# A third pair of k tiles by seven products in every second gate/up chunk, and the mixer's block transfers issued from SyncE

## The chip, the cores and the metric

The kernel runs on one core of a Trainium2 chip. The metric is device time in microseconds (us) of one execution. The core's engines are TensorE (PE in the profile; PEld its weight loads), VectorE (DVE), ScalarE (ACT), GpSimd (POOL) and SyncE (SP); each takes its instructions in the order in which the program lists them.

## The reference

One decoder layer on 256 positions of width 2048, all in float32:

```
x = x + 0.5 * swiglu(rms_norm(x, ffn1_norm), w_gate, w_up, w_down)      # 2048 -> 5632 -> 2048
h = rms_norm(x, mix_norm); proj = h @ w_in                               # 2048 -> 11776
dq, dk, dv, fq, fk, fv, g_dil, g_diff = split(proj)
o_dil  = mix of three dilated causal attention groups (4 heads each)
o_diff = causal differential attention (4 heads), normed
y = sigmoid(g_dil) * (o_dil @ W_A) + sigmoid(g_diff) * (o_diff @ W_B)
x = x + y @ w_out
x = x + 0.5 * swiglu(rms_norm(x, ffn2_norm), w_gate2, w_up2, w_down2)

def swiglu(h, w_gate, w_up, w_down):
    return (jax.nn.silu(h @ w_gate) * (h @ w_up)) @ w_down
```

## The kernel before

**Products in three parts.** TensorE multiplies in a rounded format. So each operand is split into a high part and a low part, and a product is three matmuls: high by high, high by low, low by high (`three`, L146 to L152). The activations `xh`, `xl` lie split in SBUF, 16 k tiles of 128. Weights come from memory in `raw` tiles of two k tiles by 512 columns (512 KB), loaded by SyncE; ScalarE writes the high part `w_hi` (L110, L125), VectorE subtracts it to get `w_lo` (L111, L126). There are five pairs of `w_hi` and `w_lo` buffers (`SPL_BUFS`), four `raw` buffers, and two more inside the feed-forward networks. A buffer is free when TensorE has done the matmuls that read it.

**Feed-forward.** Gate and up have 5632 columns: 11 chunks of 512, six in the first half and five in the second, each half followed by its share of the down product. Chunk 0 is done by `linear`, gate after up. Chunks 1 to 10 are done by `two_chunks` (L176): gate and up of a chunk together, over 8 pairs u of k tiles. A plain pair takes 8 products (2 k tiles, 2 blocks of 128 positions, 2 columns), from two split tiles of 1024 elements a partition. For the pairs in `sx` the 2 by 2 block product is done with seven products instead (a Winograd form of Strassen's scheme). They need sums of x, made once by `sums_of_x` (L154), and sums of weights, made at once on VectorE:

```
            b = parts(raw[0])
            three(p1, op(0, 0), part(b, 0), st, sp)
            three(c00, op(1, 0), part(b, 1), False, False)
            b = parts(raw[1][:, 1:], 1)
            three(c01, sm(3), part(b, 0), False, False)
            ... four subtractions on VectorE, in place in raw (L217 to L220)
            b = parts(raw[0])
            three(p5, sm(0), part(b, 0), st, sp)
            three(c10, op(1, 1), part(b, 1), False, False)
            b = parts(raw[1])
            three(p7, sm(2), part(b, 0), st, sp)
            three(p6, sm(1), part(b, 1), st, sp)
```

So such a pair has four split tiles: the first with 6 matmuls, the second (half a tile, 512 elements) with 3, the third and fourth, of the sums, with 6 each. `WINO = (3, 5)` names these pairs for gate and up, `WINO_DOWN = (3, 6)` those of the down product. After the last such pair four VectorE adds join the p sums (L231 to L234), after the chunk four more join the accumulators (L236); then come the gate products (L387) and two block transposes (L279). All eight PSUM banks are used, and chunks swap their roles.

**Transposing through memory.** The result of a chunk has to be turned so that its columns become k tiles. `turn_blocks` (L273) transposes 32 by 32 blocks on VectorE, writes them to memory (`blocks<-turned`, L281) and reads them back in another order (L284, into `moved`, or `q`, `fk`, `dk` in the mixer), both from GpSimd's queue. The read-back waits for the write to land. `split_blocks`, or `arrange` for the queries (L597), then takes it up some groups of weights later (`defer`).

**Mixer.** `qk_chunk` (L560) projects, norms and rotates queries and keys and turns them by `turn_blocks`; `turn_y` (L809) and `residual` (L408) do so for the mixer's output and for the new x. Their weights go through `linear`, and the norms need a power on GpSimd (L246).

**Order.** The program is written once through; a scheduler with a model of the engines' times then sets the order on each engine. So a change of the pairs also changes where VectorE's and ScalarE's other work stands.

Of the kernel before, what the change touches and what calls it, by code (L numbers as in the profile page):

```python
# [11 lines left out]
F32 = mybir.dt.float32  # L12
# [3 lines left out]
ALU = mybir.AluOpType  # L16
# [15 lines left out]
SPL_BUFS = 5  # L32
FFN_SPL = 0
FFN_RAW = 2
WINO = (3, 5)
WINO_DOWN = (3, 6)
HALVES = (6, 5)
DIL_G, DIL_H = 3, 4
# [17 lines left out]
def hybrid_layer_kernel(ctx: ExitStack, tc: tile.TileContext, a: dict, out: bass.AP):  # L56
# [94 lines left out]
        nc.tensor.matmul(ps, h, wl, start=False, stop=False)  # L151
        nc.tensor.matmul(ps, l, wh, start=False, stop=stop)  # L152

    def sums_of_x(pool, pairs, xh, xl, name):  # L154


        sx = {}
        for u in pairs:
            f = raw_tile()
            x, sm = f[:, 0].rearrange("p (k s) -> p k s", s=S), f[:, 1].rearrange("p (i m) -> p i m", m=P)  # L160
            nc.vector.tensor_tensor(x, xh[:, 2 * u:2 * u + 2].bitcast(F32), xl[:, 2 * u:2 * u + 2].bitcast(F32),
                                    op=ALU.add)
            a00, a01, a10, a11 = x[:, 0, :P], x[:, 1, :P], x[:, 0, P:], x[:, 1, P:]
            nc.vector.tensor_tensor(sm[:, 0], a10, a11, op=ALU.add)
            nc.vector.tensor_tensor(sm[:, 1], sm[:, 0], a00, op=ALU.subtract)
            nc.vector.tensor_tensor(sm[:, 2], a10, a00, op=ALU.subtract)
            nc.vector.tensor_tensor(sm[:, 3], a01, sm[:, 1], op=ALU.subtract)
            h, l = pool.tile([P, 4, P], F32R, name=f"{name}_h{u}"), pool.tile([P, 4, P], F32R, name=f"{name}_l{u}")
            nc.scalar.activation(h, sm, AF.Copy)
            nc.vector.tensor_tensor(l, sm, h.bitcast(F32), op=ALU.subtract)  # L170
            sx[u] = h, l
        return sx

    roles = itertools.count()
# [1 line left out]
    def two_chunks(cols, xh, xl, nk, sx, tmp):  # L176

        four = [ps_mm.tile([P, CH], F32, name="mm") for _ in range(4)]

        def other():
            tr = [ps_tr.tile([P, 2, S], F32, name="tr").rearrange("p a b -> p (a b)") for _ in range(2)]
            sc = ps_s.tile([P, 2, CH], F32, name="s")
            return [*tr, sc[:, 0], sc[:, 1]]

        (c00, c01, c10, c11), (p1, p5, p6, p7) = (four, other()) if next(roles) % 2 else (other(), four)
        c = ((c00, c01), (c10, c11))
        e, u2, x, y = (tmp.tile([P, CH], F32, name=n) for n in ("e", "u2", "x", "y"))  # L190
        nu, first_sum, last_sum = nk // 2, min(sx), max(sx)
        for u in range(nu):
            raw = []
            for w, n0 in cols:
                r = raw_tile()
                nc.sync.dma_start(r, w[2 * u * P:(2 * u + 2) * P, n0:n0 + CH].rearrange("(k p) n -> p k n", p=P))
                raw.append(r)
            op = lambda k, t: (xh[:, 2 * u + k, t * P:(t + 1) * P], xl[:, 2 * u + k, t * P:(t + 1) * P])
            if u not in sx:
                for i in range(2):  # L200
                    hi, lo = parts(raw[i])
                    for k in range(2):
                        for t in range(NT):
                            three(c[t][i], op(k, t), (hi[:, k], lo[:, k]), u == 0 and k == 0, u == nu - 1 and k == 1)
                    tick()
                continue
            st, sp = u == first_sum, u == last_sum
            sm = lambda i: (sx[u][0][:, i], sx[u][1][:, i])
            part = lambda hl, k: (hl[0][:, k], hl[1][:, k])

            (b00, b10), (b01, b11) = ([r[:, k] for k in range(2)] for r in raw)
# [5 lines that stand above are left out]
            nc.vector.tensor_tensor(b00, b01, b00, op=ALU.subtract)  # L217
            nc.vector.tensor_tensor(b01, b01, b11, op=ALU.subtract)
            nc.vector.tensor_tensor(b11, b11, b00, op=ALU.subtract)
            nc.vector.tensor_tensor(b10, b10, b11, op=ALU.subtract)  # L220
            tick()
# [6 lines that stand above are left out]
            tick()  # L228
            if sp:
                nc.scalar.activation(e, p1, AF.Copy)  # L230
                nc.vector.tensor_tensor(u2, p6, e, op=ALU.add)  # L231
                nc.vector.tensor_tensor(x, p5, u2, op=ALU.add)
                nc.vector.tensor_tensor(u2, p7, u2, op=ALU.add)
                nc.vector.tensor_tensor(y, p7, x, op=ALU.add)  # L234
        for acc, p in ((e, c00), (u2, c10), (x, c01), (y, c11)):
            nc.vector.tensor_tensor(acc, p, acc, op=ALU.add)  # L236
        return (e, x), (u2, y)
# [32 lines left out]
                for b in range(2):  # L270
                    split(xh[:, k + b], xl[:, k + b], tr[:, b], gains[:, k + b:k + b + 1])

    def turn_blocks(srcs, pool, x=None):  # L273

        r = pool.tile([P, 4, NT, 4, 32], F32, name="turned")
        for t in range(NT):
            nc.vector.transpose(r[:, :, t], srcs[t].rearrange("p (kt i q) -> p q kt i", i=32, q=4))  # L279
        d = dram.tile([4, P, NT * P], F32, name="blocks")  # L280
        nc.gpsimd.dma_start(d.rearrange("a (i q) x -> (a i) q x", q=4), r.rearrange("p q t kt j -> p q (t kt j)"))  # L281
        if x is None:
            x = pool.tile([P, 4, NT, 4, 32], F32, name="moved")
        nc.gpsimd.dma_start(x.rearrange("p a t kt j -> p a (t kt j)"), d.rearrange("a p x -> p a x"))  # L284
        return x

    def split_blocks(x, xh, xl, k0, gains=None):
# [73 lines left out]
    def ffn(wg, wu, wd, norm, done, ahead=None):  # L361
        with tc.tile_pool(name="act", bufs=1) as apool, tc.tile_pool(name="actw", bufs=1) as aw, \
                tc.tile_pool(name="actb", bufs=1) as bp, tc.tile_pool(name="acts", bufs=1) as sxp, \
                tc.tile_pool(name="actt", bufs=FFN_RAW) as wt, ExitStack() as spl:
            more_raw.append(wt)
            more_spl.append(spl)
            ah = apool.tile([P, 4 * HALVES[0], S], F32R, name="ah")
            al = apool.tile([P, 4 * HALVES[0], S], F32R, name="al")
            j = 0
            for half, count in enumerate(HALVES):  # L370
                down = wd[j * CH:(j + count) * CH]
                for i in range(count):
                    if j == 0:
                        ps = linear(wg, 0, xh, xl, KD, ahead)
                        rs = norm()
                        sg = [aw.tile([P, CH], F32, name=n) for n in ("e", "u2")]
                        for t in range(NT):
                            nc.scalar.activation(sg[t], ps[t], AF.Silu, scale=rs[t])
                        up = linear(wu, 0, xh, xl, KD)
                        sx = sums_of_x(sxp, WINO, xh, xl, "sx")  # L380
                    else:
                        out = two_chunks(((wg, j * CH), (wu, j * CH)), xh, xl, KD, sx, aw)
                        sg, up = [o[0] for o in out], [o[1] for o in out]
                        for t in range(NT):
                            nc.scalar.activation(sg[t], sg[t], AF.Silu, scale=rs[t])
                    for t in range(NT):
                        nc.vector.scalar_tensor_tensor(sg[t], up[t], rs[t], sg[t], op0=ALU.mult, op1=ALU.mult)  # L387
                    x = turn_blocks(sg, bp)
                    defer(BLOCK_WAIT, lambda x=x, i=i: split_blocks(x, ah, al, 4 * i))
                    j += 1  # L390
                sd = sums_of_x(sxp, WINO_DOWN, ah, al, "sd")
                for n in range(0, D // CH, 2):
                    if half and n == D // CH - 2:
                        break
                    y = two_chunks([(down, (n + c) * CH) for c in range(2)], ah, al, 4 * count, sd, aw)
                    for c in range(2):
                        (done if half else part)(n + c, [o[c] for o in y], bp)
                for n in range(D // CH - 2 if half else D // CH, D // CH):
                    done(n, linear(down, n * CH, ah, al, 4 * count), bp)
            more_spl.clear()  # L400
            more_raw.clear()
# [467 lines left out]
```

## Time and profile before

| | |
|---|---|
| runs (us) | 2123.31, 2119.55, 2126.64; median 2123.31 |
| profiled execution | 2119.51 us, span 2117.7 us |
| TensorE busy | 2102.6 us (99%), 9334 matmuls |
| VectorE busy | 1589.1 us (75%) |
| ScalarE busy | 1082.5 us (51%) |
| GpSimd busy | 100.2 us (5%) |
| weights and the rest from memory | 215 GB/s over the span |

TensorE is busy throughout; a kernel like this gets shorter by fewer matmuls or by fewer pauses of TensorE. A busy share of VectorE is a mean over stages: the feed-forward networks stand at about 50 to 720 and 1450 to 2118 us of the span, the mixer between them.

### The profile page before, as it was taken

The page shows a single profiled execution, that of the slowest core. Times are in us where ns is not written, and L with a number is a line of the kernel's source. Part 1 is how long each engine was busy: PE and PEld are TensorE (multiplying, and loading weights), DVE is VectorE, ACT ScalarE, POOL GpSimd, SP SyncE. Part 2 cuts the span into 40 slices and gives each one's busy share as a digit, 9 for nine tenths or more (in the row PEclk, how much of TensorE's full clock was granted, in tenths as well). Part 3 has the DMA queues.
Part 4 walks back from the last instruction along what each step waited for, and adds up shares of the span by engine and source line. Part 5 has one row for each costly group of instructions (what it writes and reads, how often), then busy time and mean ns, then how long its engine had stood idle before and what let it go on. Part 6 is the DMA issues. An engine that isn't in the chain of part 4 may idle for free.

```text
span 2117.7 us, 25700 instructions
## 1 busy us (share of the span) xinstructions
PE 2102.6 (99%) x9334; PEld 1736.9 (82%) x9334; DVE 1589.1 (75%) x2048; ACT 1082.5 (51%) x1335; POOL 100.2 (5%) x132
## 2 busy tenths in 40 slices
PE   9999999999999999999999999999999999999999
PEld 7888888888888888878888888888888888888887
DVE  6888987688898666677755556666898877888883
ACT  6555554455455545465555444554554544455542
POOL 1000000000000011011100000000000000000000
PEclk9999999999999999999999999999999999999999
DMA  8666665576668676766555667665676656567673
GB/s 282 218 216 210 224 236 188 186 242 227 215 209 275 224 232 196 237 190 216 192 188 159 207 223 250 228 224 179 227 241 214 210 207 218 196 218 233 207 251 125
DMA packets 224836, 456.29 MB, mean 215 GB/s; under 512 B 14098, under 2 KB 14660, under 8 KB 224452
## 3 DMA queue, kind: packets, MB, share of 16 engines
q1 hardware_dynamic: 212512, 411.09, 58.5%
q0 software_dynamic: 12096, 43.52, 6.4%
q8 instruction: 73, 1.20, 0.2%
q14 instruction: 55, 0.45, 0.1%
q10 hardware_dynamic: 100, 0.03, 0.0%
HBM read 428.89 MB, written 25.69 MB: 215 GB/s over the span
## 4 chain that ended last, share of the span: by engine, by line
PE 94%; DMA 2%; DVE 2%; ACT 1%; issue 1%; POOL 0%; ACTq 0%; POOLq 0%; DVEq 0%
PE mm L141 12%; PE mm L142 12%; PE mm L143 12%; PE mm L151 9%; PE mm L152 9%; PE mm L150 9%; PE tr L151 5%; PE tr L152 5%; PE tr L150 5%; PE s L150 5%; PE s L151 5%; PE s L152 5%; DMA q<-blocks 1%; DMA blocks<-turned 1%; DVE w_lo L126 1%
## 5 line engine op out<-in xcount | busy, mean ns | idle before, releaser
L110 ACT ACTIVATE w_hi<-raw 128x1024 fp32r<-128x1024 f32 (+1 forms) x560 | 553.0, 1016 | 540.8 <-DVE raw L220 183.7
L111 DVE TENSOR_TENSOR w_lo<-raw,w_hi 128x1024 fp32r<-128x1024 f32 (+1 forms) x560 | 639.4, 1170 | 163.1 <-ACT w_hi L110 161.0
L126 DVE TENSOR_TENSOR w_lo<-raw,w_hi 128x1024 fp32r<-128x1024 f32 (+1 forms) x313 | 378.9, 1218 | 259.5 <-ACT w_hi L125 256.6
L125 ACT ACTIVATE w_hi<-raw 128x1024 fp32r<-128x1024 f32 (+1 forms) x313 | 328.3, 1056 | 300.4 <-PE mm L143 250.0
L141 PE MATMUL mm<-w_hi,xh 128*128 128x512 f32 x864 | 339.2, 394 | 0.0
L142 PE MATMUL mm<-w_lo,xh 128*128 128x512 f32 x864 | 338.9, 393 | 0.0
L143 PE MATMUL mm<-w_hi,xl 128*128 128x512 f32 x864 | 336.7, 393 | 0.0
L151 PE MATMUL mm<-w_lo,xh 128*128 128x512 f32 x540 | 210.2, 389 | 0.0
L152 PE MATMUL mm<-w_hi,xl 128*128 128x512 f32 x540 | 210.1, 389 | 0.0
L150 PE MATMUL mm<-w_hi,xh 128*128 128x512 f32 x540 | 201.0, 389 | 0.0
L142 PEld LDWEIGHTS mm<-w_lo,xh 128*128 128x128 f32 x864 | 162.8, 188 | 33.5
L141 PEld LDWEIGHTS mm<-w_hi,xh 128*128 128x128 f32 x864 | 162.7, 188 | 33.6 <-ACT xh L255 0.2
L143 PEld LDWEIGHTS mm<-w_hi,xl 128*128 128x128 f32 x864 | 162.5, 188 | 33.6 <-DVE xl L256 0.2
L150 PEld LDWEIGHTS mm<-w_hi,xh 128*128 128x128 f32 x540 | 101.3, 188 | 21.1
L151 PEld LDWEIGHTS mm<-w_lo,xh 128*128 128x128 f32 x540 | 101.4, 188 | 21.0
L152 PEld LDWEIGHTS mm<-w_hi,xl 128*128 128x128 f32 x540 | 101.4, 188 | 21.0
L151 PE MATMUL tr<-w_lo,xh 128*128 128x512 f32 x280 | 108.9, 389 | 0.0
L150 PE MATMUL tr<-w_hi,xh 128*128 128x512 f32 x280 | 108.9, 389 | 0.0
L152 PE MATMUL tr<-w_hi,xl 128*128 128x512 f32 x280 | 108.9, 389 | 0.0
L151 PE MATMUL s<-w_lo,xh 128*128 128x512 f32 x260 | 101.1, 389 | 0.0
L150 PE MATMUL s<-w_hi,xh 128*128 128x512 f32 x260 | 101.1, 389 | 0.0
L152 PE MATMUL s<-w_hi,xl 128*128 128x512 f32 x260 | 101.1, 389 | 0.0
(280 smaller groups left out, 3240.3 us busy)
## 6 DMA issues: line engine op xcount, KB each, us to landing
raw<-in_w_in_dram SPq DMA_DIRECT2D x184, 512.0 KB, 4.1
raw<-in_ffn_w_up_dram SPq DMA_DIRECT2D x176, 512.0 KB, 4.9
raw<-in_ffn_w_down_dram SPq DMA_DIRECT2D x176, 512.0 KB, 5.4
raw<-in_ffn_w_gate_dram SPq DMA_DIRECT2D x175, 512.0 KB, 4.5
blocks<-turned POOLq DMA_DIRECT2D x41, 512.0 KB, 3.9
raw<-in_w_out_dram SPq DMA_DIRECT2D x32, 512.0 KB, 5.1
moved<-blocks POOLq DMA_DIRECT2D x31, 512.0 KB, 4.3
raw<-in_w_diff_branch_dram SPq DMA_DIRECT2D x16, 512.0 KB, 5.3
```

The source lines that it names most:

```text
L110: last_hi = nc.scalar.activation(hi[:, :n], src, AF.Copy)
L111: last_lo = nc.vector.tensor_tensor(lo[:, :n], src, hi[:, :n].bitcast(F32), op=ALU.subtract)
L125: last_hi = nc.scalar.activation(hi[:, ks], raw[:, ks], AF.Copy)
L126: last_lo = nc.vector.tensor_tensor(lo[:, ks], raw[:, ks], hi[:, ks].bitcast(F32), op=ALU.subtract)
L141: nc.tensor.matmul(ps[t], xh[:, k, sl], hi[:, kk], start=k == 0, stop=False)
L142: nc.tensor.matmul(ps[t], xh[:, k, sl], lo[:, kk], start=False, stop=False)
L143: nc.tensor.matmul(ps[t], xl[:, k, sl], hi[:, kk], start=False, stop=k == nk - 1)
L150: nc.tensor.matmul(ps, h, wh, start=start, stop=False)
L151: nc.tensor.matmul(ps, h, wl, start=False, stop=False)
L152: nc.tensor.matmul(ps, l, wh, start=False, stop=stop)
```

## The change

`WINO` gets three pairs, 2, 4 and 5. Chunks with an odd number use all three, those with an even number (from 2 on) only 4 and 5. So chunks 1, 3, 5, 7 and 9 of each network have one pair more by seven products. For pairs 4 and 5, which every chunk from 1 on does this way, the fourth sum of x isn't kept in a tile of its own: its split is written over the block of `xh`, `xl` that these pairs no longer read. `turn_blocks` takes a queue: the feed-forward's chunks keep GpSimd's, all other callers now use SyncE's, 19 writes and 19 read-backs.

```
-WINO = (3, 5)
+WINO = (2, 4, 5)
...
-            h, l = pool.tile([P, 4, P], F32R, name=f"{name}_h{u}"), pool.tile([P, 4, P], F32R, name=f"{name}_l{u}")
-            nc.scalar.activation(h, sm, AF.Copy)
-            nc.vector.tensor_tensor(l, sm, h.bitcast(F32), op=ALU.subtract)
-            sx[u] = h, l
+            n = 3 if u in over else 4
+            h, l = pool.tile([P, n, P], F32R, name=f"{name}_h{i}"), pool.tile([P, n, P], F32R, name=f"{name}_l{i}")
+            split(h, l, sm[:, :n])
+            sx[u] = [(h[:, i], l[:, i]) for i in range(n)]
+            if u in over:
+                sx[u].append((xh[:, 2 * u, P:], xl[:, 2 * u, P:]))
+                split(*sx[u][3], sm[:, 3])
...
-            sm = lambda i: (sx[u][0][:, i], sx[u][1][:, i])
+            sm = lambda i: sx[u][i]
...
-    def turn_blocks(srcs, pool, x=None):
+    def turn_blocks(srcs, pool, x=None, queue=None):
...
+        queue = queue or nc.sync
...
-        nc.gpsimd.dma_start(d.rearrange("a (i q) x -> (a i) q x", q=4), r.rearrange("p q t kt j -> p q (t kt j)"))
+        queue.dma_start(d.rearrange("a (i q) x -> (a i) q x", q=4), r.rearrange("p q t kt j -> p q (t kt j)"))
...
-        nc.gpsimd.dma_start(x.rearrange("p a t kt j -> p a (t kt j)"), d.rearrange("a p x -> p a x"))
+        queue.dma_start(x.rearrange("p a t kt j -> p a (t kt j)"), d.rearrange("a p x -> p a x"))
...
-                        sx = sums_of_x(sxp, WINO, xh, xl, "sx")
+                        sx = sums_of_x(sxp, WINO, xh, xl, "sx", WINO[-2:])
...
-                        out = two_chunks(((wg, j * CH), (wu, j * CH)), xh, xl, KD, sx, aw)
+                        out = two_chunks(((wg, j * CH), (wu, j * CH)), xh, xl, KD,
+                                         {u: sx[u] for u in WINO[1 - j % 2:]}, aw)
...
-                    x = turn_blocks(sg, bp)
+                    x = turn_blocks(sg, bp, queue=nc.gpsimd)
```

VectorE, chunk 3 of the first network, before: from the half tile of pair 3 to the subtractions of pair 5. `w_lo<-raw` are the low parts (512 is the half tile), `raw<-raw` the subtractions, `al` the turned activations' low part.

```order
L111 TENSOR_TENSOR w_lo<-raw,w_hi 128x512
L218 TENSOR_TENSOR raw<-raw 128x512
L219 TENSOR_TENSOR raw<-raw 128x512
L220 TENSOR_TENSOR raw<-raw 128x512
L111 TENSOR_TENSOR w_lo<-raw,w_hi 128x1024 x2
L253 TENSOR_TENSOR al<-moved,ah 128x4x128 x2
L111 TENSOR_TENSOR w_lo<-raw,w_hi 128x1024 x3
L111 TENSOR_TENSOR w_lo<-raw,w_hi 128x512
L217 TENSOR_TENSOR raw<-raw 128x512
L218 TENSOR_TENSOR raw<-raw 128x512
L219 TENSOR_TENSOR raw<-raw 128x512
L220 TENSOR_TENSOR raw<-raw 128x512
```

Here five low parts stand between the two sets of subtractions. The same chunk now, from the half tile of pair 4 to the subtractions of pair 5 (pair 2's stand ahead of this piece; lines are 4 higher):

```order
L111 TENSOR_TENSOR w_lo<-raw,w_hi 128x512
L257 TENSOR_TENSOR al<-moved,ah 128x4x128 x2
L221 TENSOR_TENSOR raw<-raw 128x512
L222 TENSOR_TENSOR raw<-raw 128x512
L223 TENSOR_TENSOR raw<-raw 128x512
L224 TENSOR_TENSOR raw<-raw 128x512
L111 TENSOR_TENSOR w_lo<-raw,w_hi 128x1024 x3
L111 TENSOR_TENSOR w_lo<-raw,w_hi 128x512
L221 TENSOR_TENSOR raw<-raw 128x512
L222 TENSOR_TENSOR raw<-raw 128x512
L223 TENSOR_TENSOR raw<-raw 128x512
L224 TENSOR_TENSOR raw<-raw 128x512
```

Between the two sets stand three full low parts and the half one, and the activations' low parts are ahead of both.

SyncE at the beginning of the mixer, before: the weight loads follow each other, but for the stores of x.

```order
L416 DMA x_mid<-xs 128x2x512
L123 DMA raw<-in_w_in_dram 128x2x512 x8
L416 DMA x_mid<-xs 128x2x512
L123 DMA raw<-in_w_in_dram 128x2x512 x152
L123 DMA raw<-in_w_dil_branch_dram 128x2x512 x2
```

Now, the first query and key chunks:

```order
L123 DMA raw<-in_w_in_dram 128x2x512 x13
L286 DMA blocks<-turned 128x1024
L123 DMA raw<-in_w_in_dram 128x2x512
L289 DMA q<-blocks 128x4x256
L123 DMA raw<-in_w_in_dram 128x2x512 x7
L286 DMA blocks<-turned 128x1024
L123 DMA raw<-in_w_in_dram 128x2x512
L289 DMA fk<-blocks 128x4x256
L123 DMA raw<-in_w_in_dram 128x2x512 x15
```

Write and read-back of a chunk stand in SyncE's row of weight loads, with one load between them.

## Rows read from the trace of the kernel before

**Rows 1.** The page, parts 1 and 4: busy time by engine, the chain's shares.

```profile
PE 2102.6 (99%) x9334; PEld 1736.9 (82%) x9334; DVE 1589.1 (75%) x2048; ACT 1082.5 (51%) x1335; POOL 100.2 (5%) x132
...
PE 94%; DMA 2%; DVE 2%; ACT 1%; issue 1%; POOL 0%; ACTq 0%; POOLq 0%; DVEq 0%
```

**Rows 2.** Stretches: from:to, length, VectorE busy (instructions), granted clock, DMA, GB/s.

```profile
97.80:139.90 42.10, 38.89 (x82) 1.00 0.69 227
...
417.04:501.36 84.32, 73.98 (x85) 1.00 0.68 222
```

**Rows 3.** Timeline of TensorE in chunk 7: start, length, instruction.

```profile
466.29 0.39 PE L152 MATMUL tr<-w_hi,sx_l 128*128 128x512 f32 x1
466.52 0.39 PE L150 MATMUL mm<-w_hi,sx_h 128*128 128x512 f32 x1
```

**Rows 4.** Timeline of ScalarE there; in brackets idle time before and its releaser.

```profile
462.84 3.18 ACT L110 ACTIVATE w_hi<-raw 128x1024 fp32r<-128x1024 f32 x3 [4.33 <-DVE raw L220]
465.92 0.58 ACT L230 ACTIVATE e<-mm 128x512 f32<-128x512 f32 x1
```

**Rows 5.** Timeline of VectorE, chunk 6's end into chunk 7.

```profile
437.74 0.68 DVE L236 TENSOR_TENSOR x<-mm,x 128x512 f32<-128x512 f32 x1
...
438.94 0.74 DVE L387 SCALAR_TENSOR_TENSOR e<-x,rr,e 128x512 f32<-128x512 f32 x1
439.60 1.22 DVE L111 TENSOR_TENSOR w_lo<-raw,w_hi 128x1024 fp32r<-128x1024 f32 x1
...
442.42 1.05 DVE L279 STREAM_TRANSPOSE turned<-u 128x512 f32<-128x512 f32 x1
443.38 1.19 DVE L111 TENSOR_TENSOR w_lo<-raw,w_hi 128x1024 fp32r<-128x1024 f32 x1
...
447.34 0.69 DVE L111 TENSOR_TENSOR w_lo<-raw,w_hi 128x512 fp32r<-128x512 f32 x1
448.06 0.69 DVE L219 TENSOR_TENSOR raw<-raw 128x512 f32<-128x512 f32 x1
...
452.41 1.29 DVE L253 TENSOR_TENSOR al<-moved,ah 128x512 fp32r<-128x512 f32 x2 [0.49 <-ACT ah L252]
...
459.86 0.69 DVE L217 TENSOR_TENSOR raw<-raw 128x512 f32<-128x512 f32 x1
...
463.93 7.05 DVE L111 TENSOR_TENSOR w_lo<-raw,w_hi 128x1024 fp32r<-128x1024 f32 x6 [1.21 <-ACT w_hi L110]
470.89 0.69 DVE L231 TENSOR_TENSOR u<-mm,e 128x512 f32<-128x512 f32 x1
```

**Rows 6.** Timeline of TensorE, first down product of the first network.

```profile
301.25 0.50 PE L150 MATMUL tr<-w_hi,sd_h 128*128 128x512 f32 x1 [0.26 <-ACT w_hi L110]
...
302.19 0.50 PE L150 MATMUL s<-w_hi,sd_h 128*128 128x512 f32 x1 [0.21 <-ACT w_hi L110]
```

**Rows 7.** Timeline of TensorE in the mixer.

```profile
904.07 0.39 PE L142 MATMUL mm<-w_lo,xh 128*128 128x512 f32 x1
906.04 1.13 PE L675 MATMUL s<-fv,at 128*128 128x256 f32 x4 [1.58 <-ACT on L680]
...
915.71 0.55 PE L688 MATMUL tr<-ident,on 128*128 128x128 f32 x3 [0.94 <-ACT on L680]
```

**Rows 8.** Timeline of ScalarE in the mixer.

```profile
900.54 1.15 ACT L597 ACTIVATE dq<-q 128x512 f32<-128x512 f32 x2 [7.49 <-DMA q<-blocks]
```

**Rows 9.** SyncE's waits, 700 to 1440 us: in total, times, longest.

```profile
SPq L123 <- DVE w_lo L126: 519.4, 215, 11.3
```

**Rows 10.** The page, part 6: issues, KB each, us to landing.

```profile
raw<-in_w_in_dram SPq DMA_DIRECT2D x184, 512.0 KB, 4.1
...
blocks<-turned POOLq DMA_DIRECT2D x41, 512.0 KB, 3.9
```

**Rows 11.** Timeline of TensorE at the kernel's start.

```profile
8.66 0.63 PE L143 MATMUL mm<-w_hi,xl 128*128 128x512 f32 x1
9.09 0.63 PE L142 MATMUL mm<-w_lo,xh 128*128 128x512 f32 x1
```

More of the change, by code (lines that the diff above doesn't have):

```diff
@@ L152, in three, with sums_of_x @@
         nc.tensor.matmul(ps, l, wh, start=False, stop=stop)
-    def sums_of_x(pool, pairs, xh, xl, name):
+    def sums_of_x(pool, pairs, xh, xl, name, over=()):
         sx = {}
-        for u in pairs:
+        for i, u in enumerate(pairs):
             f = raw_tile()
```

## The prediction

> **What bounds the kernel now.** I read the page first. TensorE is busy 99% of the span and the chain that ended last lies 94% on it [rows 1], so time is TensorE's matmuls plus its rare pauses. Back-to-back matmuls of 512 columns start 0.227 us apart (466.29 to 466.52) [rows 3]; the 0.39 in the rows is one matmul's length, which overlaps the next. A matmul taken away is therefore worth 0.227, if TensorE finds its next operand ready.
>
> Second, the stretches by chunk. Two chunks of gate and up in the first network take 84.32 us, and VectorE is busy 73.98 of them (88%); in the chunk that also builds masks it is 38.89 of 42.10 [rows 2]. The page's 75% hides this. So the reader is to look at who feeds TensorE there.
>
> Third, the timelines of one pair by seven products. I call one split weight tile a tile: ScalarE writes its high part, VectorE its low part, five buffers. A plain pair has 2 tiles of 12 matmuls (5.44 us of TensorE). A pair by seven products has 4 tiles, of 6, 3 (half a tile), 6 and 6 matmuls: 4.76 us. Between its second and third tile stand four subtractions on VectorE. They take 2.98 until ScalarE starts the third tile (459.86 to 462.84) [rows 4, 5], and VectorE gets on only at 463.93, 4.07 after the first subtraction. A full low part costs VectorE 1.16 in a row of six (463.93 to 470.89), the half one 0.72 (447.34 to 448.06). One such pair thus holds VectorE for 3 x 1.16 + 0.72 + 4.07 = 8.3 us against 4.76 on TensorE. It is paid from the lead that plain pairs give back (2.3 against 5.44). How much lead is left: the third tile's high part is done at 462.84 + 1.06 = 463.90, and TensorE wants it at 466.52 [rows 3]: 2.62 us, in pair 5, with plain pair 4 standing between it and pair 3.
>
> **The change, part by part.** The sum is made against the profiled execution (2119.5 us, span 2117.7); the median of the runs shown is 3.8 above it.
>
> Matmuls taken away: chunks 1, 3, 5, 7 and 9 of each network get a third pair, 10 in all, each 21 matmuls for 24. 30 x 0.227 = -6.8 us. This is sure as work, not as time.
>
> Even chunks (pairs 4 and 5 instead of 3 and 5). The plain pair between the two is gone; the order of VectorE shows their rows one behind the other. Count from 0, when TensorE finishes the last plain tile before pair 4. Pair 5's first tile needs that tile's buffer: ScalarE 0.1 to 1.2, VectorE to 2.35. Its second tile needs the buffer of pair 4's first (TensorE done at 1.36), so VectorE comes to it next, to 3.1. Subtractions: ScalarE starts the third tile at 6.05 and ends it at 7.1. TensorE wants it after 30 matmuls, at 6.80: 0.3 late. The fourth tile's high part comes 1.03 later (three in 462.84 to 465.92), TensorE wants it 0.45 later: another 0.6. So 0.9 a chunk, 10 chunks, +9 us. The measured lead says the same: 2.62 + 2.32 (two low parts fewer) - 5.44 = -0.5 for the third tile. Bounds 0.2 to 1.5 a chunk.
>
> Odd chunks (pairs 2, 4 and 5). Pair 2 begins one plain pair earlier after the chunk before has ended, when VectorE still closes that chunk. Count from 0 at the end of pair 1; the chunk before ended at -10.9. From -10.7 VectorE runs, in the new order: two accumulations 1.2 (437.74 to 438.94) [rows 5], a low part 1.16, two gate products 1.32 (0.66 each, 438.94 to 439.60), a subtraction and the half part 1.44, two transposes 1.92 (0.96, 442.42 to 443.38), three subtractions 2.2: to -1.5, and ScalarE's third tile of pair 2 to -0.3. Five low parts 5.8, the half part 0.72, the activations' low parts 1.3 (452.41): 7.5. Pair 4's subtractions and ScalarE 4.07: 11.6, where TensorE wants that tile at 12.24, still in time. Three low parts 3.48 and a half 0.72: 15.8. Pair 5's subtractions 2.98, ScalarE 1.06: 19.9. TensorE wants this tile after pairs 2, 3, 4 and nine matmuls, 4.76 + 5.44 + 4.76 + 2.04 = 17.0. 2.9 late, and 0.6 for the fourth tile: 3.5 a chunk, 10 chunks, +35 us. VectorE has no gap in this walk but the ones behind the subtractions, so nothing can be pulled ahead. Bounds 1.4 (if the closing work and the activations' parts fall into those gaps) to 4.5. After it four plain tiles follow, and the lead is back before the next pair 4, so the stalls add and don't spread.
>
> That TensorE does stop for a high part has a precedent: at 301.25 and 302.19, first tile of the down product's sums, it waits twice for L110 [rows 6], the third and fourth tile's pattern.
>
> Chunks with more on VectorE: masks, rotary tables and lambda in chunks 1 and 2 of the first network (38.89 against 36.99 in the mean of the two), the down product's sums in the last chunks of each half. Some 6 chunks with 1 us more: +6, bounds 0 and 12.
>
> The third pair's sums of x and their longer split (two ScalarE and two VectorE instructions more for the two overwritten blocks) fall into chunk 0, whose splits need half of VectorE; cost 0, bound +3. The overwritten half blocks aren't read by TensorE after chunk 0, and the writes wait for tiles whose buffers the next splits await anyway.
>
> The mixer's transfers: 19 pairs leave GpSimd's queue for SyncE's. On SyncE the read-back now waits for the write to land, with one weight load between them and seven or more behind it. Landings are 3.9 us for such a write and 4.1 for a weight load [rows 10]; the wait of the read-back is thus some 5 us, while a weight load is wanted four tiles (10.9 us) after its issue and takes 4.1: 6.8 to spare. SyncE waits for VectorE most of the time there anyway (519.4 us in 215 waits) [rows 9]. What can be won is TensorE's pauses there, 1.58 before 906.04 and 0.94 before 915.71 [rows 7]. They follow from ScalarE standing 7.49 us for the q read-back [rows 8], which the new queue also has to carry, so I take less than half of them, -1; bounds -3 (both gone, a little more elsewhere) and +15 (five q read-backs 3 us later each). The Trainium skill (DMA: Bandwidth & Descriptors, Specifications) gives a first-byte latency of about 1 us on GpSimd's path and 0.6 on SyncE's. By it each of the two transfers in a chain would be 0.4 sooner, an estimate of 0.8 off the stand of 7.49; the landings in this trace, 3.9 on GpSimd's queue and 4.1 on SyncE's, don't show it.
>
> Sum: -6.8 + 9 + 35 + 6 - 1 = +42.2, so 2161.7 in the scale of the profiled execution, about 2165 in that of the median.
>
> **Rivals.**
> 1. The lead carries it: buffers hide all of VectorE's extra work and TensorE keeps to its matmuls. For it: TensorE waits nowhere in such chunks now. Against: 8.3 to 4.76 and only five buffers. Time 2123.3 - 6.8 - 1 = 2115, faster.
> 2. VectorE bounds only by its total: stalls as large as its excess over two chunks. 73.98 + four gaps of 1.21 (before 463.93) [rows 5] + one pair's extra (8.3 - 2.3) = 84.8, where two chunks take 84.32 now. Ten times 0.5, less 1: 2127, hardly a change. Against: lead can't be stored beyond five buffers, so the slack of an even chunk doesn't pay an odd one's debt.
> 3. The pauses also slow TensorE's clock. Its matmuls at the kernel's start begin 0.43 apart instead of 0.227 [rows 11], half the rate, for about 10 of them: some 2 us a time. If each odd chunk's pause brought that, 10 x 2 = +20: 2185. Against: the pause of 1.58 us before 906.04 left the matmuls after it at the same spacing and the stretches show a granted clock of 1.00. The Trainium skill (TensorE: Matmul & The Clock Gate, HAM oscillation) says that idle gaps let the clock drop to 1.2 GHz; the pauses that this trace holds do not show it.
> 4. SyncE's queue becomes the mixer's wait: the read-backs behind a held weight load come late, ScalarE stands in its order for them, and TensorE runs out after some 9 us of lead. From then on each microsecond counts: +15 on top, 2180.
>
> **How the numbers follow.** Forecast 0.64, rival 1 0.07, rival 2 0.09, rival 3 0.08, rival 4 0.12. The likeliest alone: with the lower bounds, 0.2 + 1.4 a pair of chunks and nothing else, -6.8 + 16 - 1 = +8, so 2131; with 1.5 + 4.5 and 12, +64, so 2187. The range of 2127 to 2190 leaves out rival 1, part of rival 2 and the top of rivals 3 and 4. What can be told from no change is about 0.3%, 6 us: slower (above 2130) 0.86, within 0.07, faster 0.07.
>
> **What would show it.** Right: in odd chunks TensorE stops for L110 once or twice at pair 5, 2 to 4 us together, in even ones under 1.5; VectorE's busy share of an odd chunk rises to over 95%; matmuls fall by 30. Wrong: no waits of TensorE for ScalarE in the chunks and odd chunks of 41.5 us; or pauses at pair 2 or 4 instead of 5; or the difference lying in the mixer's stretch.

## The result: 2176.5 us, 2.5% slower, and the profile after

The changed kernel takes 2176.53 us (median of four runs, 2175.28 to 2178.12), the kernel before 2124.97 beside it: ratio 1.0253, 95% interval 1.0232 to 1.0274. The forecast was 2165 in a range of 2127 to 2190. The profiled span went from 2117.7 to 2176.3 us, 58.6 more; that is 7 more than the medians' difference, since the execution profiled before (2119.51 us) is as fast as the fastest of its kernel there and the one after (2178.12) the slowest of its four.

The page, parts 1 and 4 [rows 1]:

```profile
PE 2122.9 (98%) x9304; PEld 1738.1 (80%) x9304; DVE 1634.7 (75%) x2124; ACT 1099.5 (51%) x1361; POOL 79.2 (4%) x94
...
PE 68%; DVE 17%; issue 6%; DMA 5%; ACT 3%; POOL 0%; ACTq 0%; DVEq 0%; POOLq 0%
```

30 matmuls fewer, and yet a longer span: TensorE's share of the chain fell from 94 to 68%, and VectorE has 17% of it. What TensorE waits for (in total, times, longest):

```profile
PE mm L150 <- ACT w_hi L110: 22.4, 24, 2.5
PE tr L150 <- ACT w_hi L110: 17.0, 10, 2.5
...
PE s L150 <- ACT w_hi L110: 2.4, 11, 0.2
PE s L728 <- DMA dk<-blocks: 2.0, 1, 2.0
```

The first three, the waits for a tile's high part in products by seven, are 41.8 us together now. Before they were 1.7, this line the longest of them:

```profile
PE mm L150 <- ACT w_hi L110: 1.0, 4, 0.4
```

One even and one odd chunk (from:to, length, then busy time of PE, PEld, VectorE, ScalarE, GpSimd, granted clock) [rows 2]:

```profile
412.05:454.91 42.86, 41.92 (x184) 34.00 (x182) 33.11 (x39) 20.38 (x23) 0.00 (x0) 1.00 0.56 182
454.91:499.85 44.94, 42.34 (x179) 34.23 (x178) 40.09 (x48) 22.94 (x27) 1.30 (x2) 0.96 0.62 210
```

87.8 us for the two in place of 84.32. TensorE in pair 5, first of the even chunk, then of the odd one, with the third tile of the odd chunk's pair 4 (478.03) between them [rows 3]:

```profile
439.49 0.39 PE L152 MATMUL mm<-w_hi,xl 128*128 128x512 f32 x1
440.61 0.50 PE L150 MATMUL tr<-w_hi,sx_h 128*128 128x512 f32 x1 [0.73 <-ACT w_hi L110]
...
441.56 0.49 PE L150 MATMUL s<-w_hi,sx_h 128*128 128x512 f32 x1 [0.21 <-ACT w_hi L110]
...
478.03 0.39 PE L150 MATMUL mm<-w_hi,sx_h 128*128 128x512 f32 x1
...
482.56 0.39 PE L152 MATMUL tr<-w_hi,xl 128*128 128x512 f32 x1
485.33 0.50 PE L150 MATMUL mm<-w_hi,sx_h 128*128 128x512 f32 x1 [2.38 <-ACT w_hi L110]
...
486.28 0.95 PE L150 MATMUL mm<-w_hi,sx_h 128*128 128x512 f32 x2 [0.22 <-ACT w_hi L110]
487.03 0.63 PE L151 MATMUL mm<-w_lo,sx_h 128*128 128x512 f32 x1
487.46 0.63 PE L152 MATMUL mm<-w_hi,sx_l 128*128 128x512 f32 x1
```

Two things stand there. The third tile comes 0.89 late in the even chunk (439.49 to 440.61, less the ordinary 0.23) and 2.54 late in the odd one, the fourth some 0.4 late in both. And behind the long pause matmuls start 0.43 apart (487.03 to 487.46) instead of 0.227: TensorE runs at the lower of its two levels, 1.2 GHz. There are nine such stretches; the one above (length, PE busy, granted clock, DMA share, GB/s):

```profile
486.33:489.74 3.41, 3.41 (x9) 0.54 0.55 177
```

9 matmuls in 3.41 us where 15 would fit cost 6 x 0.227 = 1.4 us a stretch, some 12 in all. Seven stand behind an odd chunk's pause (2.35 to 2.66 us; three pauses of that size left the clock alone), one behind a pause of 2.0 and one behind one of 1.5; none stands behind a pause of 0.89.

ScalarE and VectorE ahead of the odd chunk's pause [rows 4, 5]:

```profile
470.48 1.15 ACT L256 ACTIVATE ah<-moved 128x512 fp32r<-128x512 f32 x2 [1.04 <-DMA moved<-blocks]
...
476.15 3.48 ACT L110 ACTIVATE w_hi<-raw 128x1024 fp32r<-128x1024 f32 x4 [3.99 <-DVE raw L224]
...
484.22 2.01 ACT L110 ACTIVATE w_hi<-raw 128x1024 fp32r<-128x1024 f32 x2 [1.54 <-DVE raw L224]
```

```profile
465.68 5.76 DVE L111 TENSOR_TENSOR w_lo<-raw,w_hi 128x1024 fp32r<-128x1024 f32 x5 [1.21 <-ACT w_hi L110]
471.37 1.28 DVE L257 TENSOR_TENSOR al<-moved,ah 128x512 fp32r<-128x512 f32 x2
...
473.18 0.68 DVE L221 TENSOR_TENSOR raw<-raw 128x512 f32<-128x512 f32 x1
...
477.25 4.10 DVE L111 TENSOR_TENSOR w_lo<-raw,w_hi 128x1024 fp32r<-128x1024 f32 x4 [1.21 <-ACT w_hi L110]
481.26 0.68 DVE L221 TENSOR_TENSOR raw<-raw 128x512 f32<-128x512 f32 x1
```

The turned activations' blocks (L256, L257) come just ahead of pair 4's subtractions (473.18); between those and pair 5's (481.26) stand 8.1 us, of which four low parts take 4.1. Pair 5's third tile begins on ScalarE (484.22) right after its last subtraction.

In the even chunk something else stands last. L234 is ScalarE's copy of the first p sum, for the adds that join these sums; it waits for TensorE's last matmul on that sum. VectorE's last subtraction, then ScalarE from this copy on:

```profile
438.18 0.69 DVE L224 TENSOR_TENSOR raw<-raw 128x512 f32<-128x512 f32 x1
```

```profile
439.01 0.60 ACT L234 ACTIVATE e<-tr 128x512 f32<-128x512 f32 x1 [3.85 <-PE tr L152]
439.51 2.00 ACT L110 ACTIVATE w_hi<-raw 128x1024 fp32r<-128x1024 f32 x2
```

The weights' sums are ready at 438.87, but the third tile is begun at 439.51 only, behind the copy. Before, the copy stood behind three high parts (465.92, L230) [rows 4], with no idle time.

The mixer: ScalarE stands for q less long than the 7.49 of [rows 8], TensorE's two pauses of [rows 7] are gone (the one for dk grew from 1.2 to 2.0), though the write of a block lands no sooner on SyncE's queue, 4.3 against 3.9 [rows 10]:

```profile
927.71 1.15 ACT L603 ACTIVATE dq<-q 128x512 f32<-128x512 f32 x2 [5.04 <-DMA q<-blocks]
```

```profile
blocks<-turned SPq DMA_DIRECT2D x19, 512.0 KB, 4.3
```

The account of the 58.6 us, by the distances between the starts of neighbouring matmuls less 0.227 for each 512 columns: odd chunks +35.8, even ones +17.8, half clock +11.6, the down product's sums +2.1, mixer -2.4, the kernel's start +0.3, matmuls -6.8; 0.2 are left over.

### The profile page after: what moved, and what is told of

It is laid out like the page before. It is cut to its first block, busy times and chain, and to the rows that moved or that the text cites. A ratio compares the mean times of both kernels' runs of the same rounds, so it can differ in the third digit from the quotient of the medians.

```text
span 2176.3 us, 25761 instructions
## 1 busy us (share of the span) xinstructions
PE 2122.9 (98%) x9304; PEld 1738.1 (80%) x9304; DVE 1634.7 (75%) x2124; ACT 1099.5 (51%) x1361; POOL 79.2 (4%) x94
## 4 chain that ended last, share of the span: by engine, by line
PE 68%; DVE 17%; issue 6%; DMA 5%; ACT 3%; POOL 0%; ACTq 0%; DVEq 0%; POOLq 0%
PE mm L142 12%; PE mm L143 12%; PE mm L141 12%; DVE w_lo L111 7%; PE mm L150 5%; PE mm L151 5%; PE mm L152 5%; PE tr L150 3%; PE tr L151 3%; PE tr L152 3%; PE s L151 3%; PE s L152 3%; PE s L150 3%; ACT w_hi L110 2%; DMA blocks<-turned 2%
## 5 line engine op out<-in xcount | busy, mean ns | idle before, releaser
L110 ACT ACTIVATE w_hi<-raw 128x1024 fp32r<-128x1024 f32 x580 | 563.1, 1009 | 525.4 <-DVE raw L224 170.8
L111 DVE TENSOR_TENSOR w_lo<-raw,w_hi 128x1024 fp32r<-128x1024 f32 x580 | 654.1, 1161 | 185.7 <-ACT w_hi L110 184.9
L126 DVE TENSOR_TENSOR w_lo<-raw,w_hi 128x1024 fp32r<-128x1024 f32 (+1 forms) x313 | 378.8, 1217 | 250.8 <-ACT w_hi L125 248.0
L125 ACT ACTIVATE w_hi<-raw 128x1024 fp32r<-128x1024 f32 (+1 forms) x313 | 328.6, 1056 | 308.2 <-PE mm L143 249.8
L151 PE MATMUL s<-w_lo,xh 128*128 128x512 f32 x245 | 96.5, 394 | 0.0
L152 PE MATMUL s<-w_hi,xl 128*128 128x512 f32 x245 | 96.5, 394 | 0.0
L150 PE MATMUL s<-w_hi,xh 128*128 128x512 f32 x245 | 96.4, 394 | 0.0
```

The costliest lines, as they stand in the source:

```text
L110: last_hi = nc.scalar.activation(hi[:, :n], src, AF.Copy)
L111: last_lo = nc.vector.tensor_tensor(lo[:, :n], src, hi[:, :n].bitcast(F32), op=ALU.subtract)
L125: last_hi = nc.scalar.activation(hi[:, ks], raw[:, ks], AF.Copy)
L126: last_lo = nc.vector.tensor_tensor(lo[:, ks], raw[:, ks], hi[:, ks].bitcast(F32), op=ALU.subtract)
L150: nc.tensor.matmul(ps, h, wh, start=start, stop=False)
```

## The experiments

Each median is of four executions (e10 five, e5 ten); those of the kernel before, run beside them, lay between 2123.8 and 2127.0.

**e1, e2: each half alone.** e1 gives the transfers back to GpSimd; e2 gives the pairs back (no sum overwritten).

```
-        queue = queue or nc.sync           # e1
+        queue = queue or nc.gpsimd
...
-WINO = (2, 4, 5)                           # e2, in all chunks
+WINO = (3, 5)
```

> The three pairs as in the change, but the mixer's transfers back on GpSimd's queue. In the changed kernel TensorE waits 41.8 us for ScalarE's high parts in all (1.7 before), its clock drops nine times for some 1.7 us each, and the mixer's pauses are a little shorter than before. Theory A (the pairs make the whole loss, the queue is a small gain of 2 to 3 us): 2179, ratio to before 1.024 to 1.029. Rival M (the queue costs part of the loss): below 2172.

> Pairs 3 and 5 in every chunk as before, the mixer's transfers from SyncE. Theory A: 2 to 3 us less than before, 2122, ratio 0.998 to 1.000. Rival M: slower than before by 5 us or more.

Measured: e1 2188.26, ratio 1.0297 (1.0281 to 1.0312); e2 2116.99, ratio 0.996 (0.9945 to 0.9975). The pairs alone cost more than the whole change, and the queue alone makes the kernel faster than before: the best of all that ran. Its stand for q is shorter still than above:

```profile
897.32 1.16 ACT L603 ACTIVATE dq<-q 128x512 f32<-128x512 f32 x2 [4.47 <-DMA q<-blocks]
```

In e2 the waits of TensorE list none in the mixer, where before it had four, 4.2 us together. That is the gain of the profiled spans (2117.7 to 2113.3), and half of the 8.8 us between the medians. The other half lies in executions without a profile: beside e2, six of the seven of the kernel before ran at a mean granted clock of 0.998 or 0.999, the fastest at 1.000, and those of e2 at 0.999 to 1.000. So stretches at the lower clock that e2 was spared are its likely source, which no profile shows.

In e1 the mixer's wait for dk became 5 us, again with half clock behind it (1102.92 to 1103.35):

```profile
1101.90 0.80 PE L728 MATMUL s<-dk,dq 128*128 128x128 f32 x2 [5.03 <-DMA dk<-blocks]
...
1102.92 0.63 PE L142 MATMUL mm<-w_lo,xh 128*128 128x512 f32 x1
1103.35 0.63 PE L143 MATMUL mm<-w_hi,xl 128*128 128x512 f32 x1
```

So the queue is worth some 9 us without the pairs and about 10 with them.

**e3, e4: adjacency.** e3 does pairs 4 and 5 in every chunk (two pairs as before, but adjacent), e4 pairs 2, 4 and 6 (4 and 6 in even chunks).

```
-WINO = (2, 4, 5)
+WINO = (4, 5)      # e3, in all chunks
+WINO = (2, 4, 6)   # e4
```

> Pairs 4 and 5 in all chunks 1 to 10, no third pair: as many matmuls and as much VectorE work as before, only the plain pair between the two is gone. Theory A (the lead between neighbouring pairs): each of the 20 chunks pauses as the even ones of the changed kernel do, 0.9 and 0.4 us at pair 5, some 1.4 with the slow matmuls behind them: 2125 + 28 - 2 = 2151, and no drop of the clock, since no pause is as long as 2 us. Rival T (only VectorE's total work counts): no change, 2123.

> Pairs 2, 4 and 6 in odd chunks, 4 and 6 in even ones: the changed kernel's matmuls and VectorE work, but a plain pair between any two. Theory A, by the walk of the prediction: pair 4's third tile 0.6 early as there, then pair 6's at 11.6 + 2.32 + 2.32 + 1.16 + 0.72 + 2.98 + 1.06 = 22.2 where TensorE wants it at 22.4: no pause of more than 0.5, no drop of the clock, so the 6.8 us of matmuls are won: 2115 to 2121. Rival T (VectorE's total in an odd chunk, 45 us with its gaps against 41.5): some 3 us a pair of chunks, 2145 or more.

Measured: e3 2155.74, ratio 1.0138 (1.0122 to 1.0154); e4 2149.97, ratio 1.012 (1.0103 to 1.0136). In e3 16 of the 20 chunks, odd or even, pause as the even one did above, 0.89 with the copy ahead of the third tile; one of them:

```profile
482.93 0.50 PE L150 MATMUL mm<-w_hi,sx_h 128*128 128x512 f32 x1 [0.73 <-ACT w_hi L110]
483.88 0.50 PE L150 MATMUL mm<-w_hi,sx_h 128*128 128x512 f32 x1 [0.21 <-ACT w_hi L110]
```

The other four pause 1.25 to 2.56, and three stretches run at half clock (behind 2.56, 2.29 and 1.72), which was not expected. So adjacency, with the order of the engines that comes of it, costs 1.5 us in most chunks, and two adjacent pairs, without a matmul more or fewer than before, account for over half of the loss. In e4 TensorE still waits for high parts:

```profile
PE mm L150 <- ACT w_hi L110: 10.3, 18, 1.9
PE tr L150 <- ACT w_hi L110: 8.6, 6, 2.1
```

Half of the waits are gone, half stay, in odd chunks mostly at pair 4. So spacing alone was not the cure that was expected.

**e5, e6: VectorE's subtractions.** e5 leaves out those of pair 5, e6 those of pair 2; TensorE then multiplies the weights as they came, so a part of the computation is missing.

```
+            if nk != KD or u != 5:   # e6: u != 2
                 nc.vector.tensor_tensor(b00, b01, b00, op=ALU.subtract)
...
```

> The changed kernel without the four subtractions of gate and up's pair 5 (the matmuls take the weights as they came, so part of the computation is left out). Theory A, VectorE's subtractions, 2.9 us a pair, are what TensorE waits for: then pair 5 is not late, the pauses of 1.3 us in even chunks and 3 us in odd chunks go, and with them the nine stretches at half clock. The gaps taken back are about 16 + 32 + 15 us: about 2113 to 2120, no stretch at a granted clock of 0.5 in gate and up. Rival T, the seven products' reading or splitting is late whatever VectorE does: the pauses stay, 2165 or more.

> The changed kernel without the four subtractions of gate and up's pair 2 (part of the computation is left out); pairs 4 and 5, which lie next to each other, keep theirs. Theory A1, VectorE has no time to gain a lead in an odd chunk with three pairs, and pair 2's 2.9 us are what makes pair 5's third tile 2.55 us late instead of 0.89: odd chunks then look like even ones, 0.9 + 0.4 us at pair 5, and without pauses over 2 us there are hardly any drops of the clock: 2176 - 10 x 1.7 - 13, about 2146 (2140 to 2152). Rival A2, adjacency alone makes the odd chunk's pause: it stays at 2.5 us and the time within 5 us of 2176.

Measured: e5 2118.29, ratio 0.9977 (0.9965 to 0.9989); e6 2178.71, ratio 1.0263 (1.0238 to 1.0289). In e5, the chunks that were shown above run without a pause:

```profile
412.00:455.00 43.00, 43.00 (x191) 35.62 (x190) 36.24 (x41) 24.50 (x27) 1.30 (x2) 1.00 0.60 200
455.00:497.00 42.00, 42.00 (x187) 34.76 (x186) 35.23 (x40) 21.30 (x23) 1.30 (x2) 1.00 0.74 246
```

That shows the direct cause: pair 5's four subtractions, which ScalarE has to await, cost nearly all that the pairs lost; one wait of 2.8 us is left in the second network and one of 1.7 at the down product's sums. In e5 the copy L234 stands behind the third tile again, so what the subtractions and the copy cost comes back together. e6 is the surprise. Pair 2's 2.9 us on VectorE taken away change nothing in the time: the third tile of the odd chunks is still 1.83 to 2.68 late, and that of three even ones grew to about 2. The odd chunk shown above:

```profile
490.63 0.50 PE L150 MATMUL mm<-w_hi,sx_h 128*128 128x512 f32 x1 [2.12 <-ACT w_hi L110]
```

So Theory A1, that pair 2's subtractions make pair 5's tile late, falls. VectorE has idle time ahead of pair 4 there, but ScalarE now waits for a buffer that TensorE has to free:

```profile
471.55 1.06 ACT L110 ACTIVATE w_hi<-raw 128x1024 fp32r<-128x1024 f32 x1 [1.60 <-PE s L152]
```

**e7, e8: pair 2's subtractions on GpSimd,** with pairs 2, 4, 5 (e7) and 2, 4, 6 (e8).

```
+            eng = nc.gpsimd if nk == KD and u == 2 else nc.vector
+            eng.tensor_tensor(b00, b01, b00, op=ALU.subtract)
...
```

> The changed kernel with the four subtractions of gate and up's pair 2 issued on GpSimd. If GpSimd does them in the time that lies before pair 2's third tile is wanted, odd chunks look as without them on VectorE: about 2146. If they are slower there than the lead (no trace here shows GpSimd at such an operation; VectorE's take 0.72 us each), pair 2 pauses instead and the weights' buffers come free later: up to 2190. I expect 2160, the two cases about equally likely.

> Pairs 2, 4 and 6 in odd chunks, 4 and 6 in even ones, pair 2's subtractions on GpSimd. With pairs two apart and VectorE rid of 2.9 us in each odd chunk, theory A (lead and VectorE's total together) has almost no pause left: 2150 less some 20 us, about 2125 to 2130, if GpSimd keeps up; 2150 or more if it does not.

Measured: e7 2195.55, ratio 1.0344 (1.0324 to 1.0364); e8 2162.56, ratio 1.0194 (1.0173 to 1.0216): 19 and 13 us above their likes with VectorE. One of GpSimd's rows in e7, and what VectorE does behind them:

```profile
466.13 1.30 POOL L224 TENSOR_TENSOR raw<-raw 128x512 f32<-128x512 f32 x1
```

```profile
469.93 5.77 DVE L111 TENSOR_TENSOR w_lo<-raw,w_hi 128x1024 fp32r<-128x1024 f32 x5 [4.68 <-ACT w_hi L110]
```

One takes 1.3 to 1.7 us where VectorE takes 0.69, and VectorE stands 4.68 us meanwhile, since ScalarE waits for the sums in its order.

**e9, e10: the blocks' splitting later,** with pairs 2, 4, 5 (e9) and 2, 4, 6 (e10).

```
-                    defer(BLOCK_WAIT, lambda x=x, i=i: split_blocks(x, ah, al, 4 * i))
+                    defer(14, lambda x=x, i=i: split_blocks(x, ah, al, 4 * i))
```

> The changed kernel with the splitting of the activations' blocks (ah, al; L256, L257) put off from 8 groups to 14 behind its chunk, so that it stands behind pair 5's products and not ahead of pair 4's subtractions. Theory A3: in an odd chunk ScalarE stands 1.0 to 1.75 us there for the blocks' transfer, and then VectorE splits them 1.3 us, just where pair 4's third tile has only 0.1 to 1 us of lead left; that, not pair 2's subtractions, is what makes pair 5's third tile 2.5 us late. Then pair 4 keeps 2 to 3 us more, pair 5's pause in odd chunks falls to the 0.9 of even chunks, and most stretches at half clock go: 2176 - 10 x 1.6 - 13, about 2147 (2140 to 2155). Rival B, the five buffers of split weights alone set pair 5's lead behind pair 4: the pauses stay and the time lies within 5 us of 2176.

> Pairs 2, 4 and 6 (4 and 6 in even chunks) and the blocks' splitting put off to 14 groups, both together. By A3 the pauses that were left at pair 4 with pairs apart (0.7 to 1.3 us and 0.4 behind it in odd chunks) came from the blocks; with both edits the products' pauses are nearly gone, and what is left is 6.8 us of matmuls saved and the SyncE queue's gain: 2112 (2108 to 2122), at or below pairs 3 and 5 with the transfers on SyncE (2117). Rival B: what 2, 4, 6 still paused (20.8 us of waits) stays, 2145 or more.

Measured: e9 2179.73, ratio 1.0252 (1.0237 to 1.0268); e10 2152.32, ratio 1.0117 (1.0099 to 1.0135). Both came out as rival B had it, but e9 is no test: the blocks stand where they stood, ahead of pair 4's subtractions, only with a half tile between them (in the changed kernel they stand at 470.48):

```profile
469.32 0.64 ACT L256 ACTIVATE ah<-moved 128x512 fp32r<-128x512 f32 x1 [1.02 <-DMA moved<-blocks]
469.86 0.61 ACT L110 ACTIVATE w_hi<-raw 128x512 fp32r<-128x512 f32 x1
470.38 0.62 ACT L256 ACTIVATE ah<-moved 128x512 fp32r<-128x512 f32 x1
```

The order on the engines is worked out anew from readiness, and a larger wait in the program doesn't bind it. By its time e10 is e4 once more.

**e11: six buffers for the split weights** in the feed-forward networks, at the price of two of the six raw ones.

```
-FFN_SPL = 0
-FFN_RAW = 2
+FFN_SPL = 1
+FFN_RAW = 0
```

> The changed kernel with six buffers for the split weights in the feed-forward stages in place of five; the memory is taken from the raw weights' buffers there, four in place of six. Theory B: with five buffers the fourth tile of a seven-product pair is never split more than 4.8 us before it is wanted, so that no lead carries the burst of VectorE's work behind it; a sixth buffer adds 1.4 to 2.7 us of lead. Then even chunks' 0.9 us at pair 5 go, odd chunks' 2.5 us fall to 1 or less, most stretches at half clock go: about 2135 (2120 to 2150). Rival C, VectorE's work between two pairs (about 8 us for low parts and subtractions against 4.8 to 6 us of matmuls) cannot be moved by a buffer: 2170 or more. With four raw buffers ScalarE may wait for raw<-in_w_in instead; that would show as its waits on the DMA.

Measured: 2221.23, ratio 1.0438 (1.0405 to 1.047). ScalarE now waits for weights from memory:

```profile
ACT w_hi L110 <- DMA raw<-in_ffn_w_gate_dram: 101.7, 73, 5.0
ACT w_hi L110 <- DMA raw<-in_ffn_w_down_dram: 98.1, 86, 3.8
ACT w_hi L110 <- DMA raw<-in_ffn_w_up_dram: 74.8, 74, 5.2
```

274.6 us against 56.5 in the changed kernel (4.6, 40.2, 11.7). As a whole the run thus tells of raw buffers. One chunk of each network, the even one behind the first down products, still had its weights in time. ScalarE in that of the first network, and TensorE at pair 5's third tile:

```profile
450.23 0.63 ACT L110 ACTIVATE w_hi<-raw 128x512 fp32r<-128x512 f32 x1 [1.66 <-PE mm L152]
453.45 3.91 ACT L110 ACTIVATE w_hi<-raw 128x1024 fp32r<-128x1024 f32 x4 [2.59 <-DVE raw L224]
```

```profile
456.79 0.39 PE L150 MATMUL tr<-w_hi,sx_h 128*128 128x512 f32 x1
```

No bracket: the third tile is not waited for, where the same chunk paused 0.89 at 440.61 with five buffers; it is ready some 2.3 us ahead, and the copy L234 stands behind it and the fourth. So there the sixth buffer does what theory B says.

**e12: the blocks tied behind pair 5.**

```
+                    def late(x=x, i=i):
+                        with tc.issue_after(last_hi.ins), tc.issue_after(last_lo.ins):
+                            split_blocks(x, ah, al, 4 * i)
+                    defer(12, late)
```

> The changed kernel with the blocks' splitting (L256, L257) tied behind the last low part of pair 5 on ScalarE and VectorE, since a larger wait alone had not moved it on the engines. Theory A3 (the blocks' transfer and split, 2.3 to 3 us of ScalarE and VectorE ahead of pair 4's subtractions, are what makes the odd chunks' pause 2.5 us): pair 4's third tile keeps about 2.6 us of lead, pair 5 pauses 0.9 to 1.5 us, hardly a drop of the clock: 2150 (2142 to 2158). Rival B (buffers): the pauses at pair 5 stay within 0.3 us, 2170 to 2182; the blocks may besides meet the adds at the chunk's end, a few us more.

Measured: 2172.53, ratio 1.0206 (1.0169 to 1.0243), by its time rival B. This time the blocks did move; VectorE comes straight from the low parts to pair 4's subtractions, and the odd chunk shown above pauses 1.14 instead of 2.38:

```profile
466.06 6.37 DVE L111 TENSOR_TENSOR w_lo<-raw,w_hi 128x1024 fp32r<-128x1024 f32 x6 [1.21 <-ACT w_hi L110]
472.35 0.69 DVE L221 TENSOR_TENSOR raw<-raw 128x512 f32<-128x512 f32 x1
```

```profile
484.51 0.50 PE L150 MATMUL mm<-w_hi,sx_h 128*128 128x512 f32 x1 [1.14 <-ACT w_hi L110]
...
489.25 0.50 PE L151 MATMUL tr<-w_lo,xh 128*128 128x512 f32 x1 [0.35 <-DVE w_lo L111]
```

Over all odd chunks the third tile is 0.89 to 2.04 late (one 2.67), which is 0 to 1.7 less than with the blocks ahead, and four stretches of the networks run at half clock instead of nine. But most of it is lost again in waits of the last row's kind: behind pair 5 TensorE now waits for low parts, since VectorE splits the blocks there (9 waits, 6.7 us; the changed kernel has none). Both A3 and B hold in part.

## Why the prediction was right, and where its steps were not

The sign and the mechanism held: pair 5's third and fourth tile come late behind their subtractions (e5), at the place foretold, "once or twice at pair 5, 2 to 4 us together" in odd chunks. The sum of +42.2 was 16 short of the 58.6 measured; only the width of the range held the result, since a cost that the sum left out (the half clock) and one that it did not see (the copy in even chunks) came on top. By its steps:

- *30 matmuls less, -6.8*: as said.
- *Even chunks, 0.9 each, +9*: measured +17.8, 1.5 in most and up to 2.6. The third tile was taken as 0.3 late and is 0.89; the fourth's 0.38 and the short delays behind it were there. For VectorE the walk was right: the subtractions end at 438.87, and begun 0.1 later, as in the odd chunk, the tile would be 0.35 late (an estimate from these rows). What the walk lacks is the copy L234 ahead of the tile on ScalarE, the other 0.54. Six of the ten even chunks are 0.89 late by it; in the other four the subtractions end later. No run moved the copy alone. The bound of 1.5 was about the usual value, not the top.
- *Odd chunks, 3.5 each, +35*: measured +35.8 with the half clock taken out. The last leg of the walk held. From pair 4's third tile to pair 5's ScalarE takes 8.07 us (476.15 to 484.22), while TensorE wants them 4.76 apart; so 3.3 us of lead are used up. The walk had pair 4's tile 0.6 ahead; in the chunk shown it is 0.8 ahead (done at 476.15 + 1.06, wanted at 478.03), and 3.3 less 0.8 is the 2.5 measured. In all odd chunks this lead is 1.0 or less, in even ones 1.3 to 5.7. What did not hold is the reason for the small lead. The walk let VectorE run from pair 2 to pair 5 with no gap but those behind the subtractions, so that pair 2's set the delay. In the chunk shown VectorE does run so (1.21 idle ahead of 465.68 and of 477.25), but without pair 2's subtractions (e6) it has time to spare and the pause stays. And VectorE's share of the odd chunk is 40.09 of 44.94, 89%, not over 95. What the runs support instead: a pair by seven products empties its four tiles in 4.76 us, so five buffers hold less time behind it; and the blocks' transfer and split take up to 1.7 us more (e12). That the buffers limit the lead is shown in even chunks alone (e11); how the odd chunk's 2.5 us divide between buffers, blocks and VectorE's work stays open, since no run had six buffers and its weights in time.
- *Chunks with more on VectorE, +6*: 2.1 at the down sums; the mask chunk paused no longer than its likes, clock aside.
- *The mixer, -1*: -2.4 in the profile, but e2 shows 9 us for the queue by itself, beyond the bound of -3. The working looked only at the two pauses of one profile. By the first-byte latencies of the Trainium skill (DMA: Bandwidth & Descriptors, Specifications) q's stand of 7.49 would fall by an estimated 0.8. It fell to 4.47 in e2, in the same direction and by more than the start of two transfers. The read-backs of q landed in 4.3 us there (median of five) against 5.4 before; where the rest of the 3.0 comes from, no run here tells.
- *Rival 3, half clock, +20, given 0.08*: true in part, 12 us. Its "against" rested on one pause of 1.58 us; pauses of 2.4 and more had no row before. The Trainium skill (TensorE: Matmul & The Clock Gate, HAM oscillation) says that idle gaps let the clock fall, and the rows after agree, where the prediction leaned on their absence. With the 8.8 of the even chunks and 0.8 of the odd ones, less 3.9 at the sums and 1.4 in the mixer, these 11.6 make up the 16.
- *Rival 1, the lead carries it*: ruled out by the waits. *Rival 2, only the total counts*: ruled out by e3, which has nearly VectorE's work of e2 in another place and takes 39 us more. *Rival 4, SyncE's queue as the mixer's wait*: ruled out by e2.

## What to carry to other kernels

Price a unit that a second engine must prepare by the lead in time that its buffers hold: units that are used up faster than plain ones shrink it for those behind them, so moving heavy units next to each other costs even where the engine has time in total. Look at the order on the engine between, too: a copy of 0.6 us ahead of the wanted tile cost 0.5 us in most even chunks. To a forecast pause of TensorE add a slow stretch behind it where pauses of that size had one (here most of those of some 2.5 us, and one of 1.5). And measure the parts of a bundled change alone: here one of them was a gain of 0.4% that the other hid.

## What was not expected of the hardware

After pauses of about 2.5 us in the changed kernel TensorE mostly ran on at 1.2 GHz (granted 0.54 over such a stretch), after 0.89 never; pauses of one size went both ways (2.54 at 482.56 did, 2.52 at 573.28 did not). One program's executions differ in this: e10's profiled one, the fastest of its five (2145.0 us), had waits for high parts of up to 1.8 us, one of 2.2 in the mixer and a mean granted clock of 1.000; its other four ran at 0.995 to 0.998 in 2151.25 to 2155.68 us. GpSimd's subtraction of 128x512 took 1.3 to 1.7 us to VectorE's 0.69.
